# Layer two in single results, a written order for SP's loads at the opening of attention, and the gate weights on ScalarE's queue

## The chip, the cores and the metric

The kernel runs on one core of a Trainium2 chip. The metric is the device time of one execution in microseconds (us): the median of three runs. A profiled execution of the kernel before is beside it, with a time and a span of its own. In what follows PE is TensorE (the matrix engine), ACT is ScalarE, DVE is VectorE, POOL is GpSimd and SP is SyncE, which does nothing here but start DMA transfers.

## The reference

One inference step of a two-layer hybrid encoder, for a prompt of 2048 tokens and a sample of 32 tokens, 1024 channels wide. Both are worked on together as 2080 columns. Layer one is a gated delta rule, layer two attention over a sliding window, which reads keys and values that are projected once from the output of layer one.

```python
def delta_layer(x, conv_buf, s0, w_in, ...):            # layer one
    proj = x @ w_in                                     # q, k, v, z and two small inputs
    qkv, new_buf = causal_conv(proj[..., :CONV_DIM], conv_buf, conv_w)
    ...
    o, s_new = gated_delta_rule(q, k, v, g, beta, s0)   # 8 heads, 128 wide, in chunks of 64 or 128
    o = o * lax.rsqrt(jnp.mean(o * o, -1, keepdims=True) + RMS_EPS) * norm_w * jax.nn.silu(z)
    out = o.reshape(b, l, A_VW) @ w_out
    return layer_norm(DN_ALPHA * x + out, ln_g, ln_b), new_buf, s_new

def shared_kv(h, w_kv, pos):
    kv = h @ w_kv                                       # 4 heads of 64 for k and for v
    ...                                                 # k gets a partial rotation (rope)

def swa_layer(x, k, v, pos, cached, w_in, sinks, w_out, ln_g, ln_b):   # layer two
    proj = x @ w_in
    q = rope_partial(proj[..., :B_QW], pos) * (B_HD ** -0.5)           # 16 heads of 64
    z = proj[..., B_QW:]
    o = banded_attention(q, k, v, sk)                   # a chunk of 64 sees itself and two before
    out = (o * jax.nn.silu(z)) @ w_out
    return layer_norm(DN_ALPHA * x + out, ln_g, ln_b)
```

## The kernel before

All matrix products are float32 work done as three products of split numbers: each operand is a high part and a rest ("hi" and "lo", or `xs_h` and `xs_l`), and hi·hi, hi·lo and lo·hi are summed in one bank of PSUM. Token columns come in five blocks of 416.

The program runs in stages, each with tile pools of its own, one after the other on PE:

- **Projections of layer one** (class `P1`): 24 weight tiles for q, k and v over all five blocks, with the convolution and its activations on DVE and ACT behind them. Beside this, `presplit` splits the weights of later stages: a load `pre_raw`, a cast on ACT and a subtraction on DVE to `pre_hl`, and a store to scratch memory (`s_w2`, `s_wo`).
- **Gate stage** (`P1.z`, from about 583 us): the eight gate weights over the first three blocks. For each of the 24 results ACT makes a tanh (`zth`, line 321), DVE two steps (`z`, lines 322 and 323), and SP starts a store (`s_z`). A weight is loaded as `w_raw` (one buffer, line 46), cast to `w_hi` on ACT (line 53), and the rest `w_lo` comes from POOL (line 54); `split_gate` does this one head ahead and also stores both parts (`s_wz`) for a later use. The helper work for the first chunks of the delta rule runs in between.
- **Delta rule** and **output of layer one** (to about 1370 us). The result `hT` goes to scratch.
- **Projections of layer two** (class `P2`, lines 1135 to 1483; PE from about 1339 to 1811 us). The first block of 416 columns is done plainly: a *unit* is one kind (v, k, q or z) and one pair of results, with four products of 12 matmuls. The other four blocks are done as two pairs; a unit of a pair is a seven-product scheme (`winograd`; P1, P6, P5, P7, P2, P3, P4 in this order), whose right operands are sums of parts of `hT`. `load_pair(ph)` makes these for pair `ph`: for each of four k it takes four blocks `b11` to `b22`, and DVE makes four sums and seven rests `xs_l` (line 1228), ACT seven highs `xs_h` (line 1223). `both` runs it beside the ten or twelve steps of the units that come before the pair, two steps of `load_pair` for each.
- After each result comes its post work (`post`): a rope on DVE for q and k, a tanh on ACT and one step on DVE for z (`gate`), four transposes on PE for v (`turn`, line 1462). It is put off in `todo` and called by `after()`, one or two of them for each product. The result tile `ra` (four buffers) is free again when its store has landed.
- **Opening of attention** (lines 1723 to 1761; about 1760 to 1835 us). The last three plain units (q, results 2 to 7) are worked through half a product at a time, beside scores, softmax and transposes of chunks 10 to 13. `load_k` and `load_v` load keys and values (`kT`, `vp`; POOL copies parts of `vp` to `vd`), `start` the gate `zs` and the queries `qs`. While the ring of weights (12 tiles `w`) drains, `load()` fills it with the output weights of layer two (`w<-s_wo`, line 1308, on ACT's queue). Then come the pools of the output stage (`open_right`), and `ready` splits the first gated result to `g_hi` (ACT) and `g_lo` (POOL).
- **Attention** and the output projection with its normalization, to the end.

In a `manual_schedule` block the engines that it names keep the order in which the program emits; the other engines (SP among them in all blocks before) get the order that the scheduler gives them by its own costs. In the trace each engine works through its instructions in the order it was given, and the start of a DMA is one of the instructions of the engine whose queue it is on.

The places that the change and the steps of the prediction touch are the lines named above, and the program's last part:

```python
with tc.manual_schedule(engines={ET.PE, ET.DVE, ET.Activation}):
    att.load_k(8, 14)
    att.load_v(8, 14)
    loads = iter(((14, 18), (18, 24), (24, 32)))
    for i, _ in enumerate(att.opening([order.pop(0) for _ in range(4)], p2.after)):
        drain(itertools.islice(late, 1))
```

## Time and profile before

| | |
|---|---|
| median of three runs | 2170.49 us (2164.15 to 2180.5) |
| profiled execution | 2170.48 us, of which the span in the profile is 2168.7 us |
| PE busy | 2071.5 us, 96% of the span |
| PE weight loads | 1878.5 us, 87% |
| DVE busy | 1486.6 us, 69% |
| ACT busy | 908.2 us, 42% |
| POOL busy | 730.5 us, 34% |
| bytes moved by DMA | 430.28 MB, 198 GB/s over the span |

PE is the engine that the span is made of: it stands idle for 97 us in all. A "wait" is the idle time of an engine before an instruction, put down to what ended last. Beside idle time a slice also has the clock that TensorE was granted, as a share of full speed: at 0.5 a matmul takes about twice as long. In a row of time slices ("windows") the columns are the slice, its width, the busy time of PE, of its weight loads, of DVE, ACT and POOL with the number of instructions, the granted clock, the busy share of the DMA engines and GB/s. In a row of the timeline they are start, duration, engine, line and instruction with what it writes and reads, and in brackets the idle time before it with its releaser.

### The profile page before, as it was taken

The page shows a single profiled execution, that of the slowest core. Times are in us where ns is not written, and L with a number is a line of the kernel's source. Part 1 is how long each engine was busy: PE and PEld are TensorE (multiplying, and loading weights), DVE is VectorE, ACT ScalarE, POOL GpSimd, SP SyncE. Part 2 cuts the span into 40 slices and gives each one's busy share as a digit, 9 for nine tenths or more (in the row PEclk, how much of TensorE's full clock was granted, in tenths as well). Part 3 has the DMA queues.
Part 4 walks back from the last instruction along what each step waited for, and adds up shares of the span by engine and source line. Part 5 has one row for each costly group of instructions (what it writes and reads, how often), then busy time and mean ns, then how long its engine had stood idle before and what let it go on. Part 6 is the DMA issues. An engine that isn't in the chain of part 4 may idle for free.

```text
span 2168.7 us, 37339 instructions
## 1 busy us (share of the span) xinstructions
PE 2071.5 (96%) x13494; PEld 1878.5 (87%) x13494; DVE 1486.6 (69%) x2767; ACT 908.2 (42%) x2405; POOL 730.5 (34%) x1194
## 2 busy tenths in 40 slices
PE   8999999999989999999889999899999988999998
PEld 6999999999989889888777887899989976777776
DVE  5788977886557588888876665644655556676663
ACT  5545555544322476766752111311131123545552
POOL 1212211151111087878861120000000043666565
PEclk9999999999999999999999999999999999999999
DMA  7755655557764644544854685988978896242421
GB/s 282 229 182 191 218 183 179 191 185 234 260 216 159 195 151 145 158 142 143 266 158 129 200 277 170 341 288 293 296 259 293 281 296 217 79 117 71 122 76 64
DMA packets 342410, 430.28 MB, mean 198 GB/s; under 512 B 69952, under 2 KB 269984, under 8 KB 342208
## 3 DMA queue, kind: packets, MB, share of 16 engines
q1 hardware_dynamic: 304016, 304.78, 44.3%
q10 hardware_dynamic: 38208, 123.10, 16.9%
q8 instruction: 107, 1.75, 0.3%
q14 instruction: 79, 0.65, 0.1%
HBM read 269.72 MB, written 158.44 MB: 197 GB/s over the span
## 4 chain that ended last, share of the span: by engine, by line
PE 69%; DVE 14%; DMA 5%; ACT 4%; POOL 4%; issue 3%; SPq 1%; ACTq 0%; DVEq 0%; POOLq 0%
PE ps L77 8%; PE ps L79 8%; PE ps L78 7%; PE ps L1331 5%; PE ps L1330 5%; PE ps L1332 5%; PE po L1052 3%; PE po L1054 3%; PE po L1053 3%; PE po L1851 2%; PE po L1853 2%; PE po L1852 2%; PE tr L1681 2%; PE S L1603 2%; PE ot L1706 1%
## 5 line engine op out<-in xcount | busy, mean ns | idle before, releaser
L77 PE MATMUL ps<-act_hi,w_hi 128*128 128x416 f32 x1280 | 457.8, 358 | 6.8 <-DVE z L322 2.8
L79 PE MATMUL ps<-act_hi,w_lo 128*128 128x416 f32 x1280 | 450.2, 353 | 4.7 <-POOL w_lo L54 3.6
L78 PE MATMUL ps<-act_lo,w_hi 128*128 128x416 f32 x1280 | 450.7, 352 | 0.0
L77 PEld LDWEIGHTS ps<-act_hi,w_hi 128*128 128x128 f32 x1280 | 241.5, 189 | 11.2 <-DVE z L322 3.1
L79 PEld LDWEIGHTS ps<-act_hi,w_lo 128*128 128x128 f32 x1280 | 241.6, 189 | 9.5 <-POOL w_lo L54 4.7
L78 PEld LDWEIGHTS ps<-act_lo,w_hi 128*128 128x128 f32 x1280 | 242.0, 189 | 2.8
L1330 PE MATMUL ps<-xs_h,w 128*128 128x416 f32 x560 | 198.8, 355 | 7.8 <-DVE ra L1397 6.6
L54 POOL TENSOR_TENSOR w_lo<-w_raw,w_hi 128x1024 fp32r<-128x1024 f32 x32 | 81.9, 2561 | 354.8 <-ACT w_hi L53 340.8
L1331 PE MATMUL ps<-xs_l,w 128*128 128x416 f32 x560 | 199.0, 355 | 0.5 <-DVE xs_l L1228 0.5
L1332 PE MATMUL ps<-xs_h,w 128*128 128x416 f32 x560 | 197.9, 353 | 0.0
L295 DVE SCALAR_TENSOR_TENSOR y<-R,convw,y 128x2083 f32<-128x2083 f32 (+2 forms) x78 | 175.2, 2246 | 24.7 <-ACT y L293 24.5
L585 POOL TENSOR_TENSOR tm<-L,Tt 128x60 f32<-128x60 f32 (+19 forms) x375 | 133.8, 357 | 91.8 <-PE sp L760 49.5
L588 POOL TENSOR_TENSOR Tt<-Tt,tm 128x60 f32<-128x60 f32 (+19 forms) x375 | 146.3, 390 | 28.3
L1638 POOL TENSOR_TENSOR P<-P,sm 128x512 f32<-128x512 f32 (+2 forms) x126 | 103.8, 844 | 120.0 <-DVE sm L1635 111.5
L1536 POOL MEMSET vd<- 64x768 f32 (+2 forms) x10 | 7.8, 776 | 399.2 <-DVE ra L1397 398.9
L1397 DVE SCALAR_TENSOR_TENSOR ra<-ps,u 128x416 f32<-128x416 f32 x60 | 35.4, 590 | 118.2 <-PE ps L1332 102.1
L1330 PEld LDWEIGHTS ps<-xs_h,w 128*128 128x128 f32 x560 | 106.0, 189 | 10.5 <-DVE ra L1397 7.3
L1626 ACT ACTIVATE P<-S,nm 128x192 f32<-128x192 f32 (+2 forms) x260 | 105.6, 435 | 14.4 <-DVE nm L1615 14.4
L1052 PE MATMUL po<-wo,g_hi 128*128 128x512 f32 (+1 forms) x272 | 110.5, 406 | 0.9 <-DVE hT L1100 0.9
L95 ACT CAST pre_hl<-pre_raw 128x256 fp32r<-128x256 f32 x184 | 65.7, 404 | 104.4 <-DMA pre_raw<-in_b_w_z 25.8
L1331 PEld LDWEIGHTS ps<-xs_l,w 128*128 128x128 f32 x560 | 105.8, 189 | 2.1 <-DVE xs_l L1228 0.7
L1332 PEld LDWEIGHTS ps<-xs_h,w 128*128 128x128 f32 x560 | 106.5, 190 | 1.2
(313 smaller groups left out, 4750.8 us busy)
## 6 DMA issues: line engine op xcount, KB each, us to landing
w<-s_w ACTq DMA_DIRECT2D x180, 512.0 KB, 4.5
s_w<-pre_hl SPq DMA_DIRECT2D x160, 256.0 KB, 2.5
w_raw<-in_w_in SPq DMA_DIRECT2D x32, 512.0 KB, 6.7
s_wo<-pre_hl SPq DMA_DIRECT2D x64, 256.0 KB, 4.1
gb<-s_gcum SPq DMA_DIRECT2D x34, 256.0 KB, 4.9
k<-s_k SPq DMA_DIRECT2D x34, 256.0 KB, 4.2
s_z<-z SPq DMA_DIRECT2D x40, 208.0 KB, 2.0
s_q<-y SPq DMA_DIRECT2D x8, 1024.0 KB, 5.2
```

Source lines behind the costliest of these rows:

```text
L77: nc.tensor.matmul(ps, hi[:, k, :], xh[:, k, :], start=(k == 0), stop=False)
L78: nc.tensor.matmul(ps, hi[:, k, :], xl[:, k, :], start=False, stop=False)
L79: nc.tensor.matmul(ps, lo[:, k, :], xh[:, k, :], start=False, stop=(k == KC - 1))
L295: self.nc.vector.scalar_tensor_tensor(out=y[:, a:z], in0=R[:, a + j:z + j], scalar=self.convw[:, i, j:j + 1], in1=y[:, a:z], op0=ALU.mult, ...
L585: P.tensor_tensor(out=tm[:n, i0 - k:, :w], in0=L[:n, i0:, j:j + 1].to_broadcast(sh), in1=Tt[:n, j:j + 1, :w].to_broadcast(sh), op=ALU.mult)
L588: P.tensor_tensor(out=Tt[:n, i0:, :w], in0=Tt[:n, i0:, :w], in1=tm[:n, i0 - k:, :w], op=ALU.subtract)
L1052: nc.tensor.matmul(ps[:n], ghi[:, k, :n], w[0][k][:, cs], start=(k == 0), stop=False)
L1330: nc.tensor.matmul(ps, w[:, 0, k], xh[:], start=first and k == 0, stop=False, skip_group_check=True)
L1331: nc.tensor.matmul(ps, w[:, 0, k], xl[:], start=False, stop=False, skip_group_check=True)
L1332: nc.tensor.matmul(ps, w[:, 1, k], xh[:], start=False, stop=last and k == 3, skip_group_check=True)
L1626: nc.scalar.activation(P[:, u, :nk], S[:, u, :], AF.Exp, bias=nm[:, u:u + 1], scale=1.0, accum_out=sm[:, u:u + 1])
L1638: nc.gpsimd.tensor_tensor(out=out, in0=part, in1=f, op=ALU.mult)
```

## The change

It has three parts.

**Gate stage.** The loads of the gate weights (`w_raw`) go from SP's queue to ACT's. The pool for `zth` and `z` has four buffers for each in place of two. The stores `s_z` of the first three blocks go from SP's queue to ACT's too, each one result later (`lag`): behind the tanh of the next.

**Projections of layer two.** A plain unit is now one result (two products) in place of two. The sequence is: k both results, q the first, v both and z the first three; pair one; q the second and z the other five; pair two; q the other six. `load_pair` is written anew: three steps for each k in place of an opening step and two or three, with the rests `xs_l` placed behind other work; `both` gives two steps of it to each of the first four steps of the units, and then one. The gate of z is split: the step on DVE and the store come one `after()` behind the tanh. The transposes of v in the plain block come two calls later than before.

**Opening of attention.** SP is among the engines that keep the emitted order, up to and with the first chunk of the output stage. The loads `w<-s_wo` go from ACT's queue to SP's. `start` for chunks 10, 12 and 14 is called earlier, beside the loads of keys. In `ready` the tile `r` is taken ahead of `g_hi` and `g_lo`.

```diff
-def fetch_weights(nc, pool, src):
+def fetch_weights(nc, pool, src, queue=None):
...
-    nc.sync.dma_start(raw[:], src)
+    (queue or nc.sync).dma_start(raw[:], src)
...
-    def z(self, blocks, pool, tags, ps, weights):
+    def z(self, blocks, pool, tags, ps, weights, lag=False):
...
                 nc.scalar.activation(th[:], p[:, :TB], AF.Tanh, scale=0.5)
+                if late:
+                    nc.scalar.dma_start(*late)
...
-                nc.sync.dma_start(self.T["z"][h, :, b * TB:(b + 1) * TB], z[:])
+                store = self.T["z"][h, :, b * TB:(b + 1) * TB], z[:]
+                if lag:
+                    late = store
+                else:
+                    nc.sync.dma_start(*store)
...
-            raw = fetch_weights(self.nc, self.wp, self.I["w_in"][25 + h]) if h < 7 else None
+            raw = fetch_weights(self.nc, self.wp, self.I["w_in"][25 + h], self.nc.scalar) if h < 7 else None
...
+        for k in range(4):
+            b11, b12, b21, b22 = (self.staged[k][h, b] for h in range(2) for b in range(2))
             self.high("P1", k, b11)
             sum(b12, b22, b12, ALU.subtract)
             self.high("P3", k, b22)
-            self.low("P3", k, b22, V)
-            self.low("P1", k, b11, V)
+            self.high("P7", k, b12)
+            low("P1", k, b11)
             self.high("P2", k, b21)
-            self.low("P2", k, b21, V)
...
             sum(b11, b12, b11, ALU.add)
-            self.low("P7", k, b12, V)
+            yield
             self.high("P6", k, b11)
+            low("P3", k, b22)
+            low("P7", k, b12)
             sum(b22, b22, b11, ALU.subtract)
-            self.low("P6", k, b11, V)
...
+            yield
             self.high("P5", k, b22)
-            self.low("P5", k, b22, V)
+            low("P2", k, b21)
+            low("P6", k, b11)
             sum(b21, b21, b11, ALU.subtract)
             self.high("P4", k, b21)
-            self.low("P4", k, b21, V)
+            low("P5", k, b22)
+            low("P4", k, b21)
...
-                    self.nc.scalar.dma_start(flat.bitcast(F32), self.T["wo"][1][slot // 2, :, slot % 2])
+                    self.nc.sync.dma_start(flat.bitcast(F32), self.T["wo"][1][slot // 2, :, slot % 2])
...
             nc.scalar.activation(s[:], a[:], AF.Tanh)
+            return lambda: times(s)
+
+        def times(s):
             V.scalar_tensor_tensor(out=a[:], in0=s[:], scalar=1.0, in1=a[:], op0=ALU.add, op1=ALU.mult)
...
-        self.todo.append({"z": gate, "v": lambda: turn}.get(kind, rope))
+        def wait():
+            return turn if t0 else lambda: lambda: turn()
+
+        self.todo.append({"z": gate, "v": wait}.get(kind, rope))
...
+        r = pool.tile([128, D], F32, tag="r", name="r")
         ghi = pool.tile([128, KC, 128], F32R, tag="g_hi", name="g_hi")
...
-    zp = new_pool(tc, left, "p1_z", 2, side="left")
+    zp = new_pool(tc, left, "p1_z", 4, side="left")
...
-        for _ in a:
-            drain(itertools.islice(b, 2))
+        for i, _ in enumerate(a):
+            drain(itertools.islice(b, 2 if i < 4 else 1))
...
-    sequence = [("z", j, 0) for j in range(4)] + [p + (1,) for p in pairs]
-    sequence += [("v", 0, 0), ("k", 0, 0), ("q", 0, 0)] + [p + (2,) for p in pairs]
-    sequence += [("q", j, 0) for j in range(1, 4)]
+    def halves(*of):
+        return [(kind, n // 2, 0, n % 2) for kind, a, z in of for n in range(a, z)]
+
+    sequence = halves(("k", 0, 2), ("q", 0, 1), ("v", 0, 2), ("z", 0, 3)) + [p + (1,) for p in pairs]
+    sequence += halves(("q", 1, 2), ("z", 3, 8)) + [p + (2,) for p in pairs]
+    sequence += halves(("q", 2, 8))
...
-    with tc.manual_schedule(engines={ET.PE, ET.DVE, ET.Activation}):
+    with tc.manual_schedule(engines={ET.PE, ET.DVE, ET.Activation, ET.SP}):
         att.load_k(8, 14)
         att.load_v(8, 14)
-        loads = iter(((14, 18), (18, 24), (24, 32)))
+        att.start(10)
+        loads = {8: (14, 18, 12), 14: (18, 24, 14), 20: (24, 32, None)}
...
-            if i in (8, 14, 20):
-                a, z = next(loads)
+            if i in loads:
+                a, z, n = loads[i]
                 att.load_k(a, z)
                 att.load_v(a, z)
+                if n:
+                    att.start(n)
...
+    with tc.manual_schedule(engines={ET.PE, ET.DVE, ET.Activation}):
         att.load_k(0, 8)
```

The first place is the start of the gate stage on ACT. `th` and `s_v` are the last steps of the convolution, `pre_hl` the casts of `presplit`. Before:

```order
L95 CAST pre_hl<-pre_raw 128x256 x4
L275 ACTIVATE th<-y 128x2083
L95 CAST pre_hl<-pre_raw 128x256 x4
L280 DMA s_v<-y 128x32
L321 ACTIVATE zth<-ps 128x416 x4
L53 CAST w_hi<-w_raw 128x1024
L321 ACTIVATE zth<-ps 128x416 x3
```

And now:

```order
L95 CAST pre_hl<-pre_raw 128x256 x8
L275 ACTIVATE th<-y 128x2083
L280 DMA s_v<-y 128x32
L322 ACTIVATE zth<-ps 128x416 x2
L324 DMA s_z<-z 128x416
L322 ACTIVATE zth<-ps 128x416
L324 DMA s_z<-z 128x416
L46 DMA w_raw<-in_w_in 128x1024
L322 ACTIVATE zth<-ps 128x416
L324 DMA s_z<-z 128x416
L53 CAST w_hi<-w_raw 128x1024
```

All eight casts stand ahead of `th`, and the load of the third gate weight (index 26, the one that `w_hi` in the last row is cast from) stands behind three tanh and two stores; before, it was on SP.

The second place is DVE at the end of `load_pair(1)`. `b` with a number are the blocks of the fourth k, `a<-zs,a` is the step of a gate, `ra<-ps,u` the first sum of the first pair unit (`c12`, line 1397 before), behind which PE may start P7. Before:

```order
L1249 TENSOR_TENSOR b_14558<-b_14558,b_14554 128x416
L1228 TENSOR_TENSOR xs_l<-b_14554,xs_h 128x416
L1228 TENSOR_TENSOR xs_l<-b_14558,xs_h 128x416
L1249 TENSOR_TENSOR b_14560<-b_14560,b_14554 128x416
L1228 TENSOR_TENSOR xs_l<-b_14560,xs_h 128x416
L1452 SCALAR_TENSOR_TENSOR a<-zs,a 128x416 x3
L1397 SCALAR_TENSOR_TENSOR ra<-ps,u_14802 128x416 x2
```

And now:

```order
L1237 TENSOR_TENSOR xs_l<-b_14547,xs_h 128x416
L1258 TENSOR_TENSOR b_14553<-b_14553,b_14547 128x416
L1237 TENSOR_TENSOR xs_l<-b_14551,xs_h 128x416
L1237 TENSOR_TENSOR xs_l<-b_14553,xs_h 128x416
L1451 SCALAR_TENSOR_TENSOR a<-zs,a 128x416
L1393 SCALAR_TENSOR_TENSOR ra<-ps,u_14822 128x416
L1451 SCALAR_TENSOR_TENSOR a<-zs,a 128x416
```

Before, three gates stand between the last rest and `c12`; now one, and a second behind it.

The third place is the opening of attention, on ACT and on SP. `a<-ps` copies a plain result out of PSUM, `pt<-tr` the transposed probabilities, `P,sm<-S,nm` are exponentials. ACT before:

```order
L1308 DMA w<-s_wo 128x1024
L1378 ACTIVATE a<-ps 128x416
L1308 DMA w<-s_wo 128x1024 x2
L1378 ACTIVATE a<-ps 128x416
L1683 COPY pt<-tr 128x384
L1626 ACTIVATE P,sm<-S,nm 128x192 x4
```

ACT now:

```order
L1630 ACTIVATE es<-es 128x4
L1374 ACTIVATE a<-ps 128x416 x2
L1685 COPY pt<-tr 128x384
L1628 ACTIVATE P,sm<-S,nm 128x192 x4
L1630 ACTIVATE es<-es 128x4
L1685 COPY pt<-tr 128x384
```

SP now, from the load of chunk 10's gate on:

```order
L1570 DMA zs<-s_bz 128x8x128
L1303 DMA w<-s_wo 128x1024
L1530 DMA kT<-s_bk 128x2x512
L1535 DMA vp<-s_bv 128x4x256
L1562 DMA ks<-in_cache_kT 128x2x128
L1563 DMA ks<-s_bk 128x2x32
L1565 DMA vc<-in_cache_v 128x256
L1567 DMA vn<-s_bv 32x256
L1303 DMA w<-s_wo 128x1024 x3
L1530 DMA kT<-s_bk 128x2x256
L1535 DMA vp<-s_bv 128x2x256
L1570 DMA zs<-s_bz 128x8x128
```

ACT starts no DMA there any more. On SP the loads of keys and values stand between those of the output weights, each of which needs a ring tile that PE has to free.

More of the change, by code (lines that the diff above doesn't have):

```diff
@@ L1249, in sum, with low @@
             V.tensor_tensor(out=out[:], in0=a[:], in1=b[:], op=op)
-        def quads(k):
-            return (self.staged[k][h, b] for h in range(2) for b in range(2))
-        def first(k):
-            b11, b12, b21, b22 = quads(k)
+        def low(name, k, src):
+            self.low(name, k, src, V)
+        for k in range(4):
+            b11, b12, b21, b22 = (self.staged[k][h, b] for h in range(2) for b in range(2))
             self.high("P1", k, b11)
@@ L1297, in slots @@
     def slots(self, what):
-        return sum(self.PLAIN, ()) if what[2] == 0 else self.ORDER
+        return self.PLAIN[what[3]] if what[2] == 0 else self.ORDER
     def load(self, most=2):
@@ L1346, in after @@
         for f in second:
-            f()
+            then = f()
+            if then is not None:
+                self.second.append(then)
         for _ in range(most):
@@ L1362, in plain @@
     def plain(self, unit):
-        kind, j, _ = unit
+        kind, j, _, c = unit
         nc = self.nc
         x = list(zip(*self.x0))
-        for c in range(2):
-            ps = (self.ppl or self.ppr).tile([128, 512], F32, tag="ps", name="ps")[:, :TB]
-            for h in range(2):
-                w = self.weight(unit, self.PLAIN[c][h])
-                for ks in ((0, 1), (2, 3)) if self.late else (range(4),):
-                    if ks[0] == 2:
-                        yield 1.13
-                    self.product(ps, w, x[4 * h:4 * h + 4], h == 0, h == 1, ks)
-                self.load()
-                if h == 1:
-                    pool, bufs = (self.late, 3) if self.late else (self.wk, 4)
-                    a = pool.tile([128, TB], F32, tag="ra", name="a", bufs=bufs)
-                    nc.scalar.activation(a[:], ps, AF.Copy, scale=self.SCALES[kind])
-                if not self.late:
-                    self.after()
-                if h == 1:
-                    self.post(kind, 2 * j + c, a, 0, self.cs0, 0)
-                yield 2.25
+        ps = (self.ppl or self.ppr).tile([128, 512], F32, tag="ps", name="ps")[:, :TB]
+        for h in range(2):
+            w = self.weight(unit, self.PLAIN[c][h])
+            for ks in ((0, 1), (2, 3)) if self.late else (range(4),):
+                if ks[0] == 2:
+                    yield 1.13
+                self.product(ps, w, x[4 * h:4 * h + 4], h == 0, h == 1, ks)
+            self.load()
+            if h == 1:
+                pool, bufs = (self.late, 3) if self.late else (self.wk, 4)
+                a = pool.tile([128, TB], F32, tag="ra", name="a", bufs=bufs)
+                nc.scalar.activation(a[:], ps, AF.Copy, scale=self.SCALES[kind])
+            if not self.late:
+                self.after()
+            if h == 1:
+                self.post(kind, 2 * j + c, a, 0, self.cs0, 0)
+            yield 2.25
     def winograd(self, unit):
@@ L1912, in program @@
     mid.close()
-    zp = new_pool(tc, left, "p1_z", 2, side="left")
+    zp = new_pool(tc, left, "p1_z", 4, side="left")
     chunks = [Chunk(NP, NS)] + [Chunk(t * 128, 128) for t in range(16)]
-    zs = p1.z((0, 1, 2), zp, ("zth", "z"), p1.ps, p1.gate)
+    zs = p1.z((0, 1, 2), zp, ("zth", "z"), p1.ps, p1.gate, True)
     ahead = Ahead(tc, mid, left, I, O, T, G).inverses(chunks[:2])
```

18 lines of the change are left out of this document (3 added, 15 removed).

## The prediction

> **What bounds the kernel now.** I read the page first: the busy times, then the chain of work that ended last.
>
> ```profile
> PE 2071.5 (96%) x13494; PEld 1878.5 (87%) x13494; DVE 1486.6 (69%) x2767; ACT 908.2 (42%) x2405; POOL 730.5 (34%) x1194
> PE 69%; DVE 14%; DMA 5%; ACT 4%; POOL 4%; issue 3%; SPq 1%; ACTq 0%; DVEq 0%; POOLq 0%
> ```
>
> PE is busy for 2071.5 of 2168.7 us. The change takes no matmul away, so what it can win lies in PE's 97 us of idle time and in matmuls that run at a lowered clock. The waits of PE by what released them come next.
>
> ```profile
> PE tr L1681 <- ACT pt L1683: 15.5, 3, 8.3
> PE ps L1330 <- DVE ra L1397: 6.6, 2, 3.7
> PE ps L79 <- POOL w_lo L54: 3.6, 3, 1.8
> PE ps L1462 <- ACT a L1378: 3.5, 2, 2.3
> PE ps L77 <- DVE z L322: 2.8, 1, 2.8
> ```
>
> Three columns: the sum, how many, the longest. These five belong to the three stages that the change edits: `tr` to the opening of attention, L1330 and L1462 to the projections of layer two, L77 and L79 to the gate stage. The time slices around them give what each costs, the clock included.
>
> ```profile
> 605.00:640.00 35.00, 28.57 (x141) 25.82 (x140) 11.85 (x21) 7.75 (x21) 4.73 (x2) 0.90 0.78 248
> 1390.00:1415.00 25.00, 19.52 (x91) 17.74 (x90) 10.24 (x20) 7.43 (x16) 0.00 (x0) 0.86 0.93 332
> 1565.00:1590.00 25.00, 21.53 (x109) 20.53 (x108) 21.38 (x42) 14.95 (x34) 0.00 (x0) 0.93 0.66 224
> 1600.00:1605.00 5.00, 2.33 (x12) 2.31 (x13) 1.10 (x3) 0.00 (x0) 0.00 (x0) 1.00 1.04 417
> 1770.00:1790.00 20.00, 11.62 (x51) 10.13 (x48) 11.13 (x22) 5.72 (x23) 11.37 (x19) 0.74 1.01 322
> 1815.00:1835.00 20.00, 11.70 (x55) 8.58 (x52) 6.86 (x18) 5.22 (x21) 5.80 (x6) 0.74 0.66 226
> ```
>
> For each slice I take width less PE busy as idle, and PE busy times (1 - clock) as lost to the clock. Gate stage: 6.4 + 2.9 = 9.3 us. Pair one of layer two: 5.5 + 2.7 = 8.2. Pair two, from two slices: 3.5 + 1.5 + 2.7 = 7.7. Opening of attention, first group: 8.4 + 3.0 = 11.4; second: 8.3 + 3.0 = 11.3. Together 47.9 us: this is all that the change can win at the places it edits.
>
> The clock falls behind stalls of 2.8 us (in the first row) as behind 8.3. The Trainium skill, "TensorE: Matmul & The Clock Gate", Part 1, gives half clock only after an idle window of about 3.4 us. The rows disagree for single short stalls. By that rule the short stalls that I leave below would cost no clock, and the sum would be some 2 us lower.
>
> **Gate stage: a wait removed, another put in.** The rows are from the timeline and the list of transfers.
>
> ```profile
> 597.61 1.95 ACT L275 ACTIVATE th<-y 128x2083 f32<-128x2083 f32 x1 [5.30 <-DVE y L295]
> 599.46 1.31 ACT L95 CAST pre_hl<-pre_raw 128x256 fp32r<-128x256 f32 x4
> 602.38 0.93 ACT L321 ACTIVATE zth<-ps 128x416 f32<-128x416 f32 x2 [1.61 <-DVE pre_hl L96]
> 606.16 1.04 ACT L53 CAST w_hi<-w_raw 128x1024 fp32r<-128x1024 f32 x1
> 599.59 2.33 DVE L276 SCALAR_TENSOR_TENSOR y<-th,y 128x2083 f32<-128x2083 f32 x1 [2.01 <-ACT th L275]
> 620.81 0.65 DVE L322 TENSOR_SCALAR z<-ps,nwh 128x416 f32<-128x416 f32 x1 [15.18 <-DMA s_z<-z]
> 602.41 5.41 SPq L97 DMA_DIRECT2D s_wo<-pre_hl  x4
> 614.07 0.45 SPq L324 DMA_DIRECT2D s_z<-z  x1
> 607.33 2.38 POOL L54 TENSOR_TENSOR w_lo<-w_raw,w_hi 128x1024 fp32r<-128x1024 f32 x1 [21.88 <-ACT w_hi L53]
> 609.77 0.46 PE L79 MATMUL ps<-act_hi,w_lo 128*128 128x416 f32 x1 [0.53 <-POOL w_lo L54]
> w_raw<-in_w_in SPq DMA_DIRECT2D x32, 512.0 KB, 6.7
> kT<-s_bk SPq DMA_DIRECT2D x2, 512.0 KB, 9.1
> r<-s_h SPq DMA_DIRECT2D x16, 512.0 KB, 3.5
> ```
>
> Before, DVE stands for 15.18 us because the first `s_z` starts only at 614.07, behind the `s_wo` stores and the loads that follow them on SP, and `z` has two buffers. PE fills its free banks of PSUM and then waits. With stores on ACT and four buffers this goes, and with it the later waits for `z`, `w_hi` and `w_lo`: 9.3 us.
>
> What comes: weight 26. Its load was early on SP; now it stands on ACT behind `th`, three tanh and two stores, and `th` itself behind the last four casts. These casts began at 599.46 with no wait of their own, so their load was there a little earlier; I take 598.9. Then casts 1.31, `th` 1.95, DVE's `y` 2.33 and `s_v` 0.4 make 604.9. The first tanh ends at 605.4; two DVE steps (0.65 and the like) end at 606.6; store 0.4, tanh 0.5, the second store (its `z` ends at 607.9) 0.4: `w_raw` starts at about 608.3 and is out at 608.7. Landing 6.7: 615.4. Cast 1.04, rest 2.38: 618.8. PE asks for this `w_lo` at 609.77 - 0.53 = 609.2. So it idles for about 9.6 us, and as behind the opening's stall I add 3.0 of clock: 12.6. The next weights have room: a load starts about 1.5 us behind the last tanh of a head, landing, cast and rest take 10.1, and the three blocks of the next head are 72 matmuls, 13.1 us (141 take 28.57 - 2.9 us in the first slice, 0.18 each). Net **+3.3**. With the 512 KB rows at 3.5 and 9.1 in place of 6.7 it is 0 to +6; I keep 6.7, which is the same transfer. ACT now also waits for each `z` before its store, about 1.2 us; behind it stand tanh steps, which the free PSUM banks cover, and the loads, in which it is counted.
>
> **Layer two.** DVE is the engine that PE waits for.
>
> ```profile
> 1369.88 0.29 DVE L1100 COPY hT<-ps 128x128 f32<-128x128 f32 x1 [5.79 <-PE ps L1098]
> 1370.59 0.58 DVE L1249 TENSOR_TENSOR b<-b,b 128x416 f32<-128x416 f32 x1
> 1374.00:1398.00 24.00, 22.13 (x115) 21.01 (x113) 20.80 (x41) 14.56 (x31) 0.00 (x0) 1.00 0.86 297
> 1396.60 0.59 DVE L1228 TENSOR_TENSOR xs_l<-b,xs_h 128x416 fp32r<-128x416 f32 x1 [0.61 <-ACT xs_h L1223]
> 1400.37 0.59 DVE L1452 SCALAR_TENSOR_TENSOR a<-zs,a 128x416 f32<-128x416 f32 x1 [1.70 <-ACT zs L1451]
> 1400.88 0.58 DVE L1397 SCALAR_TENSOR_TENSOR ra<-ps,u 128x416 f32<-128x416 f32 x1
> 1602.03 0.59 DVE L1397 SCALAR_TENSOR_TENSOR ra<-ps,u 128x416 f32<-128x416 f32 x1 [2.01 <-DMA s_bk<-a]
> ```
>
> 41 instructions take 20.80 us: 0.507 each. Between 1370.59 and `c12` at 1400.88 lie 49 of them, 24.8 us, so 5.5 us are waits, for `xs_h` and for tanh. In the new order 47 lie there, and three rope steps in place of a gate put the start 1.1 us later: 1371.7 + 23.8 = 1395.5 without waits, 1401.0 with all of them. PE wants `c12`'s end at 1401.52 - 3.73 = 1397.8 (the wait of 3.7 in the list), or at 1396.1 if its 1.7 us of waits on P6 go too. The rests now stand one or more instructions behind their highs and two of three tanh waits are cut by the split gate, so I take 1 us of the 5.5 as left. That makes a stall of about 1.0, 0.6 for P6 of the last k, and 0.4 of clock: 2.0 of 8.2, a saving of 6.2. The ropes of k and q ahead of it cost nothing: they lie in DVE's idle time behind row 1369.88 (5.79 us); without that cover they would put `c12` 4 us later.
>
> Pair two: v's transposes no longer fall into `load_pair`, and come two calls later: 3.5 and the clock's 1.5 go. `c12` waited there for a store of k and, before it, for four ropes; in the new sequence gates stand there, one DVE step each. I leave 1.5 of 7.7: a saving of 6.2. A gate put off by one call delays a store by one product (2.3 us) and with it a buffer of `ra`; units of k and q have had their last step there all along, and the list shows L1330 waiting on `ra` only twice in all, at the two pairs' first units. So nothing is charged. Sum **-12.4**, between -3 (all 5.5 us of waits stay, pair two keeps half) and -15.9 (nothing left).
>
> **Opening of attention.**
>
> ```profile
> 1775.66 3.17 ACTq L1308 DMA_DIRECT2D w<-s_wo  x2
> 1778.88 0.52 ACT L1378 ACTIVATE a<-ps 128x416 f32<-128x416 f32 x1 [6.99 <-DMA w<-s_wo]
> 1794.33 0.48 ACT L1683 COPY pt<-tr 128x384 f32<-128x384 f32 x1 [4.65 <-PE tr L1681]
> 1822.82 1.04 ACT L1818 CAST g_hi<-graw 128x1024 fp32r<-128x1024 f32 x1 [10.07 <-DMA s_bq<-a]
> 1782.16 2.83 POOL L1539 COPY vd<-vp 64x512 f32<-64x512 f32 x4 [1.92 <-DMA vp<-s_bv]
> 1785.08 1.96 POOL L1638 TENSOR_TENSOR P<-P,sm 128x512 f32<-128x512 f32 x2
> 1786.77 15.47 SPq L1479 DMA_DIRECT2D s_bq<-a  x4
> ```
>
> ACT stands before its `w<-s_wo` starts, and the copies of `a` and `pt` behind them; PE waits for `pt`. With the loads on SP both copies wait for PE alone. Against the move speaks the Trainium skill, "DMA: Bandwidth & Descriptors", Issuing engines are not separate DMA queues: the transfers share the same engines, and another issuer saves only the time to start them, usually small. Here the start held ACT for 3.17 us and the copy came 6.99 late, so the trace speaks for the move; what is right in the rule is a rival below.
>
> What is late next: POOL. It normalizes P (1785.08) behind copies of `vd` that wait for `vp`, and in the new order the copies of the `vp` piece of chunks 14 to 17 stand there too. With what stands ahead of it on SP from the first `kT` on, that load makes 5.7 MB by the shapes of the rows; at 322 GB/s from about 1762 on it lands at about 1780, and with copies (half of 2.83) and norm (1.96) P is there at 1783.5. PE wants it 11.4 us sooner than the row at 1794.33, at 1782.3 with the 0.6 us of the transposes. I leave 2.5 with a clock share of 1: the first group saves 8. In the second, `g_hi` no longer takes memory that an `s_bq` store still reads, but `g_lo` on POOL does, of earlier stores, and it stands behind copies of `vd` for the last `vp` piece; I leave 7, a saving of 4.3. Sum **-12.3**, between -22.7 and +16 (the slower rival).
>
> **Sum.** 2170.5 (profiled execution, equal to the median) + 3.3 - 12.4 - 12.3 = 2149.1; I say 2149.
>
> **Rivals.** *All of it hidden.* ACT works off its queue sooner or weight 26 lands in 3.5 us (gate +0), both pairs lose 1 us at most, and the opening all but 5: 2170.5 - 13.8 - 17.7 = 2139; with nothing left anywhere 2132. For it: in none of the slices is DVE or POOL full without a transfer behind it. Against: the 1.92 wait for `vp`.
>
> *Transfers bind the opening.* The slice 1770 to 1790 already has a DMA share of 1.01 at 322 GB/s, the highest row above 417. If the rate stays at 322, 20 us of bytes take 20 us, PE's stall moves to whatever lands last, and the first group saves nothing; the second, at share 0.66, keeps its 4.3. Then 2170.5 + 3.3 - 12.4 - 4.3 = 2157; with P2's low end as well 2167. This is what the page's rule above amounts to.
>
> *Slower.* SP now works in the written order, and a load of the output weights waits there for a ring tile that PE has to free. The load of `vp` behind it waits too, POOL's copies of `vd` wait for that, the norm of P behind the copies, and PE for P: a circle. The price for a group, with a tile freed at 1775.66, when ACT's second load of the row started, 1 us to the load of `vp`, landing 9.1, copies and norm 3.4: P at 1789.6 in place of 1782.3, 7.3 and 3.0 of clock. There are three pieces of `vp`; with one of the holds of 15.47 us that SP already shows it is 10.3 twice and 15.5 + 3, 39 us in place of 22.7: 2170.5 + 3.3 - 12.4 + 16.5 = 2178. It decides from about 32 us in three groups on. Against it: before, ACT's waits for those tiles were at most 3.17.
>
> **Numbers.** Forecast case 0.45 (2143 to 2156), all hidden 0.2, transfers 0.25, slower 0.1. The predicted time is the first one's. The range leaves out half of the slower case and the end of the hidden one: 2131 to 2173. A measurement of this kernel tells about 1% from no change, 21.7 us: faster means under 2148.8. All of the hidden case and somewhat over half of the forecast's own spread lie there, since its low side reaches further: 0.46. Slower by over 1%, above 2192, needs the circle in all three groups at about 18 us each: 0.05. The rest, 0.49, is within 1%.
>
> **What would show it.** Gate stage: one wait of PE of 8 to 11 us near 610 on `w_hi` or `w_lo`, and no wait of DVE on `s_z` over 3 us; if that wait of PE is under 4, this term was wrong. Layer two: L1330 on `ra` under 2.5 us in all, no L1462 on `a`. Opening: no `w<-s_wo` on ACT, no wait of `tr` on `pt` over 3 us; in its place waits of `tr` on P from POOL, of `po` on `g_lo`. The prediction is wrong if waits on POOL there exceed 10 us, or if PE's idle time moves to transfers of `kT` and `vp`.

## The result, and the profile after

| | before | after |
|---|---|---|
| median | 2168.78 us (2164.15 to 2180.5, 8 runs) | 2154.76 us (2152.04 to 2160.08, 8 runs) |
| ratio | | 0.9933, 95% interval 0.9913 to 0.9954 |
| span of the profiled execution | 2168.7 us | 2153.2 us |
| PE busy | 2071.5 us | 2060.2 us |

The change makes the kernel 0.67% faster, 14.5 us by the ratio (10 to 19). That is inside the range and 5.8 us above the predicted 2149. The terms behind the sum did less well than the sum, so the first question is where the time went. The starts of five marks on PE, read from the timeline of both executions, cut the span into stages:

| mark on PE | before | after | difference | gained since the mark above |
|---|---|---|---|---|
| first transposition of v in the delta rule | 719.4 | 724.0 | +4.6 | lost 4.6 (gate stage) |
| last transposition of layer one's output | 1369.6 | 1371.3 | +1.7 | 2.9 (no line of it is changed) |
| first scores of the opening | 1760.1 | 1755.3 | -4.8 | 6.5 (layer two) |
| first product of the output stage | 1825.6 | 1806.2 | -19.4 | 14.6 (opening) |
| first transposition of the sample's probabilities | 2025.7 | 2010.2 | -15.5 | lost 3.9 (opening's end) |
| end of the span | 2168.7 | 2153.2 | -15.5 | 0 |

The 2.9 us of the second row are how far executions differ: over all profiles of this study that stage took 646.9 to 650.6 us where nothing in it was changed. So the profile says: gate stage +4.6, layer two -6.5, opening -10.7; predicted were +3.3, -12.4 and -12.3. One profile is not exact for layer two: between the same two marks the old code took 387.5 to 390.5 us (before and runs one and three below), and the code of after 381.5 to 386.7 (eight profiles). The means, 389.0 and 385.1, are 3.9 us apart.

The waits of PE by what released them, of the kernel after, with the same three columns as before:

```profile
PE ps L77 <- ACT w_hi L53: 10.0, 2, 9.7
...
PE ps L1325 <- DVE ra L1393: 3.7, 2, 2.7
...
PE ps L79 <- POOL w_lo L54: 2.7, 2, 1.4
PE tr L1683 <- ACT pt L1685: 2.4, 1, 2.4
PE tr L1683 <- POOL P L1640: 2.2, 1, 2.2
...
PE ps L1461 <- DVE ra L1393: 1.8, 1, 1.8
...
PE ps L1461 <- ACT a L1374: 1.5, 1, 1.5
PE po L1855 <- POOL g_lo L1822: 1.0, 1, 1.0
```

The 15.5 us of `tr` behind `pt` are down to 2.4, and POOL's P and `g_lo` have come in their place (2.2 and 1.0), as named in the prediction. The waits of the pairs' first products for `ra` (6.6 before) are 3.7; 1.8 stand behind `ra` in the transposes (L1461). One wait is new and the longest of all three stages: 9.7 us on `w_hi`, weight 26.

**Gate stage.** Time slice, then the timeline of ACT, SP and PE in the kernel after:

```profile
605.00:640.00 35.00, 23.86 (x117) 22.28 (x116) 14.01 (x22) 8.24 (x19) 4.75 (x2) 0.80 0.80 257
```

```profile
600.67 1.33 ACT L95 CAST pre_hl<-pre_raw 128x256 fp32r<-128x256 f32 x4 [6.91 <-DMA pre_raw<-in_b_w_out]
601.90 1.94 ACT L275 ACTIVATE th<-y 128x2083 f32<-128x2083 f32 x1
606.68 0.93 ACT L322 ACTIVATE zth<-ps 128x416 f32<-128x416 f32 x2 [2.83 <-DVE y L276]
609.73 0.38 ACTq L324 DMA_DIRECT2D s_z<-z  x1
610.21 1.24 ACTq L46 DMA_DIRECT2D w_raw<-in_w_in  x1
612.02 0.33 ACTq L324 DMA_DIRECT2D s_z<-z  x1
617.25 1.04 ACT L53 CAST w_hi<-w_raw 128x1024 fp32r<-128x1024 f32 x1 [4.87 <-DMA s_z<-z]
618.35 0.72 PE L77 MATMUL ps<-act_hi,w_hi 128*128 128x416 f32 x1 [9.72 <-ACT w_hi L53]
620.84 0.72 PE L79 MATMUL ps<-act_hi,w_lo 128*128 128x416 f32 x1 [1.42 <-POOL w_lo L54]
```

The casts come first, `th` behind them, and the start of `w_raw` ends at 611.45, where the prediction had 608.7. The cast begins at 617.25 (predicted 615.4) and PE waits 9.7 and 1.4 us, 11.1 idle in place of 9.6. With the clock (23.86 busy at 0.80: 4.8) the slice costs 15.9 us; the slice of before cost 9.3. (The cast's row names `s_z<-z`; the semaphore that the cast itself waits for in the trace is that of the `w_raw` load started at 610.21.) The wait of 15.18 us on DVE is gone, but PE gains nothing from it.

**Layer two.** DVE, ACT and PE at the first sum of pair one, after:

```profile
1396.60 1.28 DVE L1237 TENSOR_TENSOR xs_l<-b,xs_h 128x416 fp32r<-128x416 f32 x2
1398.99 0.59 DVE L1451 SCALAR_TENSOR_TENSOR a<-zs,a 128x416 f32<-128x416 f32 x1 [1.11 <-ACT zs L1447]
1401.93 0.59 DVE L1393 SCALAR_TENSOR_TENSOR ra<-ps,u 128x416 f32<-128x416 f32 x1 [2.35 <-ACT u L1404]
1398.04 0.33 ACTq L1307 DMA_DIRECT2D w<-s_w  x1
1398.41 0.55 ACT L1447 ACTIVATE zs<-a 128x416 f32<-128x416 f32 x1 [1.15 <-DMA b<-s_hT]
1400.50 0.33 ACTq L1307 DMA_DIRECT2D w<-s_w  x1
1400.87 0.52 ACT L1374 ACTIVATE a<-ps 128x416 f32<-128x416 f32 x1 [1.91 <-DMA b<-s_hT]
1401.38 0.52 ACT L1404 ACTIVATE u<-ps 128x416 f32<-128x416 f32 x1
1402.58 0.46 PE L1325 MATMUL ps<-xs_h,w 128*128 128x416 f32 x1 [2.70 <-DVE ra L1393]
```

DVE ran through `load_pair` at 0.5 us a step without a single wait for `xs_h` and was through at 1397.9. It then stood for ACT: for a tanh and for the copy `u`. ACT did neither in time because it stood ahead of two starts of `w<-s_w`. A start first waits on the semaphore that will count its landing, until an earlier transfer on it has landed. The first start waited there for a load `b<-s_hT` that SP had started at 1391.56. For the second the row names `b<-s_hT` too, but the transfer before it on its semaphore is a `w<-s_w` of 1393.26.

### The profile page after: what moved, and what is told of

Read it like the earlier page. It is cut to its first block, busy times and chain, and to the rows that moved or that the text cites. A ratio compares the mean times of both kernels' runs of the same rounds, so it can differ in the third digit from the quotient of the medians.

```text
span 2153.2 us, 37333 instructions
## 1 busy us (share of the span) xinstructions
PE 2060.2 (96%) x13494; PEld 1869.5 (87%) x13494; DVE 1486.2 (69%) x2767; ACT 908.4 (42%) x2405; POOL 727.4 (34%) x1194
## 4 chain that ended last, share of the span: by engine, by line
PE 48%; DVE 12%; POOL 4%; DMA 3%; ACT 3%; issue 2%; SPq 0%; ACTq 0%; POOLq 0%; DVEq 0%
PE ps L1325 5%; PE ps L1326 5%; PE ps L1327 5%; PE po L1061 3%; PE po L1063 3%; PE po L1062 3%; PE po L1855 2%; PE po L1853 2%; PE po L1854 2%; POOL Tt L597 2%; POOL tm L594 2%; PE S L1605 2%; PE tr L1683 2%; PE ps L79 2%; PE ps L77 1%
## 5 line engine op out<-in xcount | busy, mean ns | idle before, releaser
L1628 ACT ACTIVATE P<-S,nm 128x192 f32<-128x192 f32 (+2 forms) x260 | 105.5, 433 | 14.6 <-DVE nm L1617 14.4
```

The source lines that it names most:

```text
L1628: nc.scalar.activation(P[:, u, :nk], S[:, u, :], AF.Exp, bias=nm[:, u:u + 1], scale=1.0, accum_out=sm[:, u:u + 1])
```

## The experiments

All are compared with the kernel before in the same series of runs; "after" stands for the changed kernel.

**1 to 3: one part alone.** Each takes the kernel before and one of the three parts of the diff.

```diff
-    zs = p1.z((0, 1, 2), zp, ("zth", "z"), p1.ps, p1.gate)
+    zs = p1.z((0, 1, 2), zp, ("zth", "z"), p1.ps, p1.gate, True)
...
-    sequence = [("z", j, 0) for j in range(4)] + [p + (1,) for p in pairs]
+    sequence = halves(("k", 0, 2), ("q", 0, 1), ("v", 0, 2), ("z", 0, 3)) + [p + (1,) for p in pairs]
...
-    with tc.manual_schedule(engines={ET.PE, ET.DVE, ET.Activation}):
+    with tc.manual_schedule(engines={ET.PE, ET.DVE, ET.Activation, ET.SP}):
```

> The kernel before with the gate stage's part alone (loads of the gate weights and stores of z on ACT's queue, four buffers). Theory: the load of weight 26 is started too late, so PE idles about 11 us near 610 to 620, against 6.4 us before, and the first product of the delta rule comes 4 to 5 us later (724 in place of 719): 2173 us. Rival: what the gate stage loses is given back by the delta rule, which waits for other things anyway: 2169, no difference.

> The kernel before with layer two's part alone (single results, new sequence, new load_pair, split gate, later transposes). Theory from the trace of the changed kernel: 6 to 7 us, 2162 to 2163 us, with a wait on the first sum of pair one of about 2.7 us left. Rival, the prediction's term: 12.4 us, 2156.

> The kernel before with the opening's part alone (SP in written order, output weights' loads on SP, start earlier, r first). Theory: about 11 us, 2158 us, ACT starts no transfer in the opening and PE's waits on pt fall from 15.5 to under 4 us. Rival: transfers bind the opening, so that it gains 4 us at most, 2165.

| | median | ratio (95%) | by the ratio |
|---|---|---|---|
| gate stage alone | 2174.06 us | 1.0014 (1.0001 to 1.0028) | +3.0 us (0 to +6) |
| layer two alone | 2164.14 us | 0.9977 (0.9964 to 0.9990) | -5.0 us (-8 to -2) |
| opening alone | 2156.39 us | 0.9943 (0.9920 to 0.9965) | -12.4 us (-17 to -8) |

The sum is -14.4 us, and the whole change gave -14.5: within their intervals the parts add. The gate stage's part costs time, its first mark, the transposition of v, comes at 724.2, and nothing of it is given back (the next stage takes 650.5 us); the rival falls. Layer two brings less than half of the 12.4 predicted (at most 8 by its interval). The opening brings what was predicted: its waits of PE, with its part alone,

```profile
PE tr L1681 <- ACT pt L1683: 2.4, 1, 2.4
PE po L1853 <- POOL g_lo L1820: 2.2, 1, 2.2
PE tr L1681 <- POOL P L1638: 1.8, 2, 1.4
```

against 15.5 on `pt` before and nothing on the other two. The rival that transfers bind the opening falls: it moves the same bytes in the time that was left.

**4: the gate weights' loads back on SP.**

```diff
-            raw = fetch_weights(self.nc, self.wp, self.I["w_in"][25 + h], self.nc.scalar) if h < 7 else None
+            raw = fetch_weights(self.nc, self.wp, self.I["w_in"][25 + h]) if h < 7 else None
```

> The changed kernel with the loads of the gate weights back on SP's queue; the stores of z stay on ACT with four buffers. Theory: the late load is the whole loss of the gate stage, and the stores and buffers are a gain: PE idles under 3 us between 605 and 640 (11.1 in the changed kernel, 6.4 before), and the time falls by 10 to 14 us to 2141 to 2145. Rival: the load is late on SP too, behind the stores and loads that stand there, or the last casts ahead of the final activation are the cause: PE still idles 6 us or more, 2150 or above.

Measured: 2155.32 us, ratio 0.9936 (0.9918 to 0.9955): no difference from after. PE still waits 9.13 us on `w_hi` at 618. So the theory fell as it stood, but not for the reason of either rival. The load starts at 586.98 on SP, and the casts are behind `th` again. Rows of ACT in this run:

```profile
602.46 0.93 ACT L322 ACTIVATE zth<-ps 128x416 f32<-128x416 f32 x2 [1.61 <-DVE pre_hl L96]
613.36 0.36 ACTq L324 DMA_DIRECT2D s_z<-z  x1
613.76 0.52 ACT L322 ACTIVATE zth<-ps 128x416 f32<-128x416 f32 x1 [10.37 <-DMA gb<-s_gcum]
616.57 0.33 ACTq L324 DMA_DIRECT2D s_z<-z  x1
616.93 1.04 ACT L53 CAST w_hi<-w_raw 128x1024 fp32r<-128x1024 f32 x1 [1.80 <-DVE z L326]
```

The first store of `z` could have started at 604.5, when its `z` was there, and starts at 613.36: it waits for a load of `gb` that SP started. The semaphores in the trace show why. In the traces of before, after and this run, all starts of SP and ACT count their landings on the same eight semaphores, which both queues use. The store on ACT waits on the one that the `gb` load also uses, and SP starts that load only at 609.29, behind its stores of `s_wo`.

On SP such a wait holds up other transfers. On ACT it holds up the tanh and the cast that PE needs.

**5 and 6: only the buffers; only the load.** The next two tell the three edits of the gate stage apart. Five takes loads and stores back to SP and keeps four buffers (the edit of run four and this one); six takes only the stores back (this one alone).

```diff
-    zs = p1.z((0, 1, 2), zp, ("zth", "z"), p1.ps, p1.gate, True)
+    zs = p1.z((0, 1, 2), zp, ("zth", "z"), p1.ps, p1.gate)
```

> The changed kernel with loads of the gate weights and stores of z back on SP, and only the four buffers for zth and z kept. Theory: what costs time in the gate stage is ACT standing before transfers that it starts (in the run before this one the cast of weight 26 stood 10.4 us behind a store of z, though its load had been there for long); with none there and four buffers, DVE's 15.2 us before z is cut by two results, PE's wait on z (2.8) and those behind it go in part, PE idles 2 to 5 us from 605 to 640 (11.1 in the changed kernel), and the time is 2144 to 2149. Rival: the stores on SP start at 614 as before, so that four buffers only move the wait: PE idles 6 us, 2150 to 2151.

> The changed kernel with the stores of z back on SP; the loads of the gate weights stay on ACT and the four buffers stay. It tells the late load apart from the stores. Theory (late load alone is enough): the load starts at about 607 to 608 behind three tanh, PE idles 7 to 10 us near 617, the time is 2152 to 2156. Rival (only the stores on ACT cost): PE idles under 4 us, 2148.

Measured: five 2147.34 us, 0.9898 (0.9883 to 0.9913); six 2151.80 us, 0.9921 (0.9907 to 0.9934). Six has the late load without the stores: PE waits 6.95 and 1.42 us near 616, the low end of what was expected, so the late load costs by itself. By the ratios it is 5 us, with intervals that just overlap. The first mark says 1.9 (718.1 in run six, 716.2 in run five); 5.1 us of the two profiles' difference lie in layer two, whose code is the same. Five is the best of the gate stage: its slice,

```profile
605.00:640.00 35.00, 30.27 (x160) 28.41 (x160) 16.59 (x23) 7.80 (x19) 7.20 (x3) 0.90 0.83 267
```

has 4.7 us of idle time against 6.4 before and 11.1 after. DVE's wait for `z` is 10.79 us there, where it was 15.18 before; what PE still waits for is a cast that stands 10.62 us for the next `w_raw` from SP. The two things that the change moved to ACT thus cost about 7.6 us of the changed kernel (0.9933 against 0.9898; 7.9 by the first mark, 724.0 against 716.2), and the four buffers are the part that helps.

**7: the output weights' loads back on ACT.**

```diff
-                    self.nc.sync.dma_start(flat.bitcast(F32), self.T["wo"][1][slot // 2, :, slot % 2])
+                    self.nc.scalar.dma_start(flat.bitcast(F32), self.T["wo"][1][slot // 2, :, slot % 2])
```

> The changed kernel with the loads of the output weights back on ACT's queue; SP's written order, the earlier start and r first stay. Theory: the loads on ACT are the cause of the first group's stall alone (11.4 us), so 9 to 11 us come back, 2164 to 2166. Rival: they are the cause of both groups, 2168 to 2170; second rival: the written order did it, 2157 or less.

Measured: 2159.46 us, 0.9957 (0.9944 to 0.9969), 5.2 us more than after by the ratios: half of what was expected, and the two intervals overlap a little. The copies on ACT wait 6.44 us again at 1773.67, behind a start whose semaphore a load of `vp` on SP still holds. But PE's waits in the first group come to 0.7 on P, 1.5 on `a` and 1.0 on `pt`, and not to the 8.4 of before; the longest, 4.5 on P, is in the second group, at 1816.18. The loads on ACT are thus not the whole of the first group's stall. Which of the opening's other edits takes the rest was not tested with the loads on ACT.

**8: layer two's weights on SP.** This puts the reading of the trace above to the test: it takes the starts of `w<-s_w` away from ACT.

```diff
-                    self.nc.scalar.dma_start(w[:].rearrange("p s k c -> p s (k c)").bitcast(F32), src)
+                    self.nc.sync.dma_start(w[:].rearrange("p s k c -> p s (k c)").bitcast(F32), src)
```

> The changed kernel with the loads of layer two's weights (w from s_w) on SP in place of ACT. Theory: what is left of PE's waits in layer two (1.5, 2.7, 1.0 and 1.8 us, and 1.5 of clock) comes from ACT, which stands before those starts (1.2 and 1.9 us near 1400 behind loads of b) with the tanh and the copy u behind it; with them on SP the wait on the first sum of pair one falls under 1 us, and the time falls by 3 to 6 us, 2149 to 2152. Rival: DVE's chain is the bound still, no change; second rival: the weights stand behind stores on SP and PE waits for them, slower by 5 us or more.

Measured: 2156.64 us, 0.9941 (0.9928 to 0.9954): no gain. Yet the theory's own place came out as it said: there is no wait of PE on `ra` any more in either pair (3.7 and 1.8 us after), only the 1.50 on a copy at 1399.28. The time was lost elsewhere, in the output stage of layer one, where the first twelve weights are loaded:

```profile
1193.27 9.16 SPq L1307 DMA_DIRECT2D w<-s_w  x9
1204.67 1.60 SPq L1307 DMA_DIRECT2D w<-s_w  x2
1217.44 1.04 ACT L1047 CAST g_hi<-g 128x1024 fp32r<-128x1024 f32 x1 [16.13 <-DMA g<-s_g]
1214.26 0.39 SPq L1039 DMA_DIRECT2D r<-in_x  x1
1218.52 1.23 DVE L1048 TENSOR_TENSOR g_lo<-g,g_hi 128x1024 fp32r<-128x1024 f32 x1 [9.96 <-ACT g_hi L1047]
1221.57 0.69 DVE L1066 SCALAR_TENSOR_TENSOR r<-r,po 128x512 f32<-128x512 f32 x1 [1.83 <-DMA r<-in_x]
```

Nine of the twelve weights in a row (512 KB each), and two more behind them, went ahead of the next loads of that stage on SP. ACT stood 16.13 us for the load of `g`, DVE 9.96 behind ACT's cast of it and then 1.83 for `r`, and PE 8.07 us at 1222.41. From the first mark to the second it takes 663.1 us, where no other profile has more than 650.6; from the second mark to the third it takes 375.8, where after took 384.0. The gain is there, and the other stage's loss hides it.

**9: both lessons together.** Loads and stores of the gate stage on SP with four buffers, and layer two's weights on SP from the first pair on, the first ring of them still on ACT.

```diff
-                    self.nc.scalar.dma_start(w[:].rearrange("p s k c -> p s (k c)").bitcast(F32), src)
+                    (self.nc.sync if self.ppl or self.late else self.nc.scalar).dma_start(w[:].rearrange("p s k c -> p s (k c)").bitcast(F32), src)
```

> The changed kernel with the gate stage's transfers on SP and four buffers kept (2147.3 us so far), and the loads of layer two's weights on SP from the first pair on only, so that the output stage of layer one, which lost 8.1 us in one wait when all of them were on SP, keeps its order. Theory: the two gains add, PE's waits on ra in layer two (3.7 us) and on the transposes there fall under 2 us together, and the time is 2141 to 2145. Rival: with the weights behind stores on SP PE waits for a weight, 2147 or more.

Measured: 2136.69 us, 0.9860 (0.9841 to 0.9879): 1.4% faster than before, and faster than after (the intervals, 0.9841 to 0.9879 and 0.9913 to 0.9954, lie apart); faster than expected too. In the place that it edits, DVE and ACT at the first sum of pair one are now

```profile
1388.66 0.58 DVE L1451 SCALAR_TENSOR_TENSOR a<-zs,a 128x416 f32<-128x416 f32 x1
1389.42 0.59 DVE L1393 SCALAR_TENSOR_TENSOR ra<-ps,u 128x416 f32<-128x416 f32 x1 [0.17 <-ACT u L1404]
1388.88 0.51 ACT L1404 ACTIVATE u<-ps 128x416 f32<-128x416 f32 x1
```

with 0.17 us of wait where 2.35 stood, and PE does not wait on `ra` at all. From the last transposition of layer one to the first scores it takes 375.8 us, the same as in run eight; it was 381.5 to 386.7 in the eight profiles with the code of after, 384.0 in after itself, and 390.5 before. The whole stage, after and in this run:

```profile
1371.29:1755.28 383.99, 375.68 (x1979) 368.75 (x1978) 216.72 (x438) 79.10 (x165) 2.22 (x4) 1.00 0.88 293
1362.15:1737.92 375.77, 373.30 (x1979) 367.43 (x1977) 216.59 (x438) 78.62 (x165) 2.22 (x4) 1.00 0.92 300
```

PE's idle time there is 2.5 us, where it was 8.3 after and 11.9 before (390.48 less 378.62). Of the 11 us to the profile of run five, 5.7 lie here; the others lie in stages whose code is the same, and differ between executions.

**10 and 11: the opening's other edits.** Ten frees SP from the written order; eleven takes `r` behind `g_hi` and `g_lo` again.

```diff
-    with tc.manual_schedule(engines={ET.PE, ET.DVE, ET.Activation, ET.SP}):
+    with tc.manual_schedule(engines={ET.PE, ET.DVE, ET.Activation}):
...
-        r = pool.tile([128, D], F32, tag="r", name="r")
         ghi = pool.tile([128, KC, 128], F32R, tag="g_hi", name="g_hi")
         glo = pool.tile([128, KC, 128], F32R, tag="g_lo", name="g_lo")
...
+        r = pool.tile([128, D], F32, tag="r", name="r")
```

> The changed kernel without SP's written order in the opening; the loads of the output weights stay on SP, the earlier start and r first stay. The scheduler then puts all loads of keys and values ahead of eleven of the twelve output weights. Theory: the gain came from taking the loads off ACT and from r, the order matters little: 2153 to 2157. Rival: the written order is worth half of it, 2159 to 2162, with longer waits of PE on P from POOL.

> The changed kernel with r taken behind g_hi and g_lo again. Theory: g_hi then takes memory that a late s_bq store still reads, ACT stands before its cast with the copy of pt behind it, as in the kernel before, and 4 to 8 us of the second group's 11.3 come back: 2159 to 2163, PE's longest wait of tr on pt 5 us or more in place of 2.4. Rival: SP's order alone made that store early enough, no change.

Measured: ten 2156.68 us, 0.9944 (0.9929 to 0.9959), 2.4 us above after, within the interval; PE's waits on P are 2.7 us, 2.2 after, and a second wait of 2.4 on `pt` has come, at 1794.02. Eleven 2158.93 us, 0.9953 (0.9939 to 0.9966), 4.3 us above after: the low end of what was expected. The intervals overlap, but the wait is the one named:

```profile
1813.13 1.04 ACT L1820 CAST g_hi<-graw 128x1024 fp32r<-128x1024 f32 x1 [11.80 <-DMA s_bq<-a]
PE tr L1683 <- ACT pt L1685: 10.0, 1, 10.0
```

One line's place decides which tile gets the memory that a store still reads: with `g_hi` in it PE waits 10.0 us, with `r` in it 2.4. (Not all of the 7.6 reach the end: the waits on `g_lo` and `r` behind it, 2.5 us after, are gone in run eleven.)

**12: load_pair and its pace as before**, in the new sequence.

```diff
-            drain(itertools.islice(b, 2 if i < 4 else 1))
+            drain(itertools.islice(b, 2))
...
-        for k in range(4):
-            b11, b12, b21, b22 = (self.staged[k][h, b] for h in range(2) for b in range(2))
+        first(0)
+        yield
+        for k in range(4):
+            second(k)
```

> The changed kernel with load_pair and its pace as before; sequence, split gate and later transposes stay. Theory: DVE gets its five waits of 0.6 us per pair back, but the first sum of pair one is held by ACT's copy u anyway, so it costs 1 to 3 us, 2156 to 2158. Rival: the rewriting carries most of layer two's gain of 5 us: 2159 to 2161.

Measured: 2168.59 us, 0.9997 (0.9983 to 1.0010), 13.9 us above after. Both guesses were far too low: with the old `load_pair` the new sequence is about 9 us slower than the old sequence was with it (13.9 less the 5.0 of run two). PE waits 13.0 us on `ra`, and DVE shows why in pair two:

```profile
1597.60 0.59 DVE L1237 TENSOR_TENSOR xs_l<-b,xs_h 128x416 fp32r<-128x416 f32 x1 [0.61 <-ACT xs_h L1232]
1611.31 0.59 DVE L1407 SCALAR_TENSOR_TENSOR ra<-ps,u 128x416 f32<-128x416 f32 x1 [5.78 <-DMA s_bz<-a]
```

The 0.61 us waits are back, the gates come late (two steps of `load_pair` to every step of the units are part of this edit), and the first sum takes a buffer of `ra` whose gate's store has to land first: 5.78 us.

## Why the prediction was right or wrong

**The sum.** Predicted 2149, range 2131 to 2173; measured 2154.76. The chance of 0.49 for "within 1%" took the case that came. The sum came near by two terms that held nearly and one that was about twice too large. Part of it is luck: by the marks the three terms together missed by 8.8 us (1.3, 5.9 and 1.6), and 2.9 of that came back in a stage of which no line was changed.

**Gate stage: right in mechanism, a little small in size.** Weight 26 on ACT behind the last casts, `th`, three tanh and two stores was the wait named, 11.1 us of idle time against 9.6, and +4.6 at the mark (+3.0 by run one) against +3.3. Two sizes were off: the start of `w_raw` itself took 1.24 us, and what is ahead of it came about 1.8 us late, since the load behind the last casts landed at 600.67 and not at 598.9. The stores on ACT were charged with 0.4 us each plus the wait for `z`. That they can also wait for a transfer of SP's queue was not in it; it is ACT's longest wait in run four (10.37 us). What the stores cost in the changed kernel stays open: 2.6 us by the ratio of run six, whose interval overlaps that of after, and 3.8 to 7.3 by the first mark (718.1 in run six, 721.9 to 725.5 in the seven profiles with the whole gate part).

**Layer two: the step that failed.** It is the sentence "I take 1 us of the 5.5 as left". The time slices around the two pairs, after, are

```profile
1385.00:1415.00 30.00, 26.74 (x138) 25.86 (x139) 16.54 (x31) 13.30 (x33) 0.00 (x0) 0.94 0.98 352
1560.00:1605.00 45.00, 42.22 (x225) 41.18 (x224) 30.94 (x60) 21.24 (x45) 0.00 (x0) 1.00 0.86 296
```

Pair one costs 4.2 us of waits (1.5 and 2.7) and 1.6 of clock, 5.8 in place of 8.2: 2.4 saved where 6.2 were forecast. Pair two costs 3.4 in place of 7.7 (1.0 on `ra`, 1.8 and 0.6 for transposes), without any of the clock: 4.3 saved where 6.2 were forecast. Together that is 6.7, near the 6.5 of the marks; run two gives 5.0 for the part alone. Both signs that the prediction named for this stage failed: the first products' waits on `ra` are 3.7 us and not under 2.5, and a transposition still waits for the copy `a` (1.5). The DVE half of the step held: no wait for `xs_h`, and `load_pair` through at 1397.9, 24.5 us behind its first sum. What was left were 3.5 us of waits for ACT, 1.11 for a tanh and 2.35 for `u`, and these come from ACT's starts of `w<-s_w`, which the prediction did not charge. The rows of before had such a wait (1.70 for a tanh); the prediction took it for ACT's work in a row and let the split gate cut it. Run eight takes the starts away and PE's waits on `ra` go to zero; run nine turns that into time. Two smaller steps failed beside it. The plain block's transposes of v had not left `load_pair` but moved from pair two's to pair one's, where one waits 1.5 us for its copy. And "nothing is charged" for the delayed gate was wrong by 1.8: in pair two DVE stood 4.83 us for a store of `z`, and transposes waited for it.

**Opening: right.** Predicted -12.3, measured -10.7 in the marks and -12.4 alone. The first group kept 2.2 us on P from POOL (predicted 2.5), the second 2.4 on `pt`, 1.0 on `g_lo` and 1.5 on `r`, 8.3 in all with the clock (6.8 us at 0.50; predicted 7). That ACT's starts hold the copies is seen again in run seven (6.44 us), and that `g_hi`'s memory holds the second group in run eleven (10.0 against 2.4 us). What they are worth in time, 5 and 4 us, is at the edge of what the intervals can tell, and run ten does not tell the written order from no effect. The earlier `start` was not tested alone.

**The rivals.** Transfers do not bind the opening. Its first stretch, after:

```profile
1765.00:1790.00 25.00, 22.82 (x144) 20.11 (x142) 18.49 (x42) 10.31 (x43) 14.15 (x22) 0.93 0.86 278
```

The share is 0.86 at 278 GB/s, and PE is busy for 22.8 of 25 us. The Trainium skill, "DMA: Bandwidth & Descriptors", Issuing engines are not separate DMA queues, says that spreading starts over engines saves only the time to start, usually small. For the transfers this agrees, since nothing here shows more bytes in less time. For the engines it does not: the same kind of start, moved from ACT to SP, was worth about 8 us of layer two in runs eight and nine (384.0 to 375.8 between the marks) and, less surely, 5.2 us in run seven, because a start waits, and work behind it waits too. The slower rival, the circle of SP, `vp`, POOL and PE, was not there: SP was through the first four output weights at 1767, while PE still worked on what came before, and the `vp` behind them started at 1768.80; POOL's wait for it did not come to PE as more than the 2.2 us on P. (Its price has a slip: 1775.66 + 1 + 9.1 + 3.4 is 1789.2 and not 1789.6, and 1775.66 is the first start of the row, not the second.) "All hidden" was wrong for the changed kernel, though run nine at 2136.7 shows that its price was not out of reach.

## What to carry to other kernels

The start of a transfer is an instruction with waits of its own, and the engine that issues it stands still for them with all the work behind it: an engine on whose copies or casts the matrix engine waits should start no transfer while earlier ones on the same semaphores are still under way, unless nothing is queued behind. When a wait on a store is to be removed, try more buffers before another queue: here the buffers alone were the faster kernel. And price a moved load by what stands ahead of it in its new queue, not by the queue's average use.

## What was not expected of the hardware

Stalls of PE well below 3 us bring the half clock: behind 2.18 us of idle time at 1779.21 the matmuls follow each other at 0.35 us, five of them, where 0.19 is the rule:

```profile
1779.21 0.90 PE L1683 MATMUL tr<-ident,P 128*128 128x128 f32 x3 [2.18 <-POOL P L1640]
1780.25 0.55 PE L1326 MATMUL ps<-x_l,w 128*128 128x416 f32 x1
1780.60 0.55 PE L1327 MATMUL ps<-x_h,w 128*128 128x416 f32 x1
1775.79:1779.20 3.41, 1.23 (x16) 0.94 (x12) 2.09 (x5) 0.00 (x0) 2.67 (x6) 1.00 1.05 405
1779.20:1782.62 3.42, 3.41 (x13) 3.21 (x13) 0.00 (x0) 2.19 (x10) 2.09 (x3) 0.50 1.07 364
```

The stall of 1.79 us at 1600.87 brought none: the slice from 1560 to 1605 has a clock of 1.00. The length of a stall alone does not decide, since a longer one, of 2.91 us at 1602.67 before, brought none either. In the traces the granted clock changes only at the borders of steps of 3.41 us, as in the last two rows. The stall of 2.18 us lies within one step; that of 2.91 is cut by a border at 1601.58 into 1.82 and 1.09. Over the fourteen traces, each step at full clock in which PE was idle for 2.0 us or more was followed by half clock (71 of 71, worked out from the clock and PE's busy times); with 1.1 to 2.0 us both happened. So the same code can lose the clock in one execution and not in another: in layer two's stage run six lost about 5 us to it (10.2 us at half clock) and run five, with the same code there, none. The Trainium skill, "TensorE: Matmul & The Clock Gate", Part 1, puts the change at an idle window of about 3.4 us; the length of the steps agrees with it, but these rows do not agree that the whole of it must be idle: 2.2 and 2.7 us were enough.
